# A hybrid decoder layer on one core: the end of its attention, with the conv branch evicted by VectorE and four pieces of work placed elsewhere

## The chip, the core and the metric

The kernel runs on one core of a Trainium2 chip. The core has a matrix engine (TensorE, PE in the profile, with its weight loads listed apart as PEld), VectorE (DVE), ScalarE (ACT), GpSimd (POOL) and SyncE (SP), which here issues nearly all transfers between the chip's main memory (HBM) and the on-chip memory (SBUF). Matrix products land in a small accumulator memory, PSUM, of eight banks of 128 x 512 float32 values; VectorE or ScalarE has to copy (evict) a bank before TensorE may write it again. Each engine works through its own list of instructions in order and waits on semaphores where it needs another's result. The metric is the device time of one execution in microseconds; lower is better.

## The reference, cut to what matters

One layer of a hybrid block on x (1024 positions, 1024 features). Two branches, attention and a gated causal convolution, are weighted by sigmoid gates, added and projected; a feed-forward block (FFN) with a convolution in it follows.

```
h = rms_norm(x, norm_mix_pre)
q, k, v, cb, cc, cx, g_att, g_conv = split(h @ w_in)       # 3 x 512, 3 x 512, 2 x 1024 columns
o = stick_breaking_attention(q, k, v)                       # 8 heads of 64, strictly causal
y_att  = o @ w_att_branch                                   # 512 -> 1024
y_conv = (cb * causal_dwconv(cc * cx, conv_mix_w)) @ w_conv_branch
merged = sigmoid(g_att) * y_att + sigmoid(g_conv) * y_conv
x = x + rms_norm(merged @ w_out, norm_mix_post)
h = rms_norm(x, norm_ffn_pre)
a, g = split(causal_dwconv(h @ w_up, conv_ffn_w))           # 2 x 2816
x = x + rms_norm((gelu(g) * a) @ w_down, norm_ffn_post)
```

In the attention the weight of a key s for a query t is exp(log_sigmoid(z) + the sum of log_sigmoid(-z) over the keys between s and t), so each block of keys needs a running sum from the blocks nearer to the query.

## The kernel before, in words

**Number format.** Every float32 operand of a product is scaled by a power of two and split into a float16 high part and a float16 low part (ScalarE writes the high part, VectorE the low part), and a product is three passes of float16 matmuls (high-high, low-high, high-low). The power of two comes from the operand's sum of squares: ScalarE squares the tile with an accumulator (`sumsq`, L58), VectorE casts the column of 128 sums to bf16 (`rb`), TensorE multiplies it by a matrix of ones (a 128 x 1 matmul into some PSUM bank), and VectorE turns the total into a scale with three tiny integer operations (`pow2_of`, L89 to L92, or `scale_of`, L78 to L81).

**The attention.** It works on units of two heads (j = 0 to 3), one half of the queries (c) and one block of 128 keys (i, downwards). A tile's name ends in the unit: `e3_11` is j = 3, c = 1, i = 1. For each unit TensorE makes scores z, ScalarE e = exp(z) (L804), VectorE bounds e (L813), ScalarE sp = log(1 + e) (L818), VectorE adds the running sum of the unit before (`sp <- A, sp`, L823), ScalarE and VectorE split sp into `sh` (L828, L832), TensorE sums it with a triangular matrix into A, ScalarE makes g = exp(-A) (L845), VectorE multiplies e by g (L849), and ScalarE and VectorE split the product into `w` (L854, L858), which TensorE multiplies by v into o. A has one PSUM buffer: the A of the next unit can be written only when g has read the last one. The last units, `3_13` to `3_10`, are the stretch of this case.

**The fills.** While that chain runs, TensorE is filled with projections that need nothing of it: q and k of the next heads, the three conv projections, the first gates gc and ga (`gate_fill`), and at the end, of the conv branch's eight output tiles d, d = 4 to 7 (`branch_fill`, `branch`, names `pywc4` to `pywc7` in PSUM, `ywc4` to `ywc7` in SBUF). Each is written into one of three PSUM banks; each bank's eviction is an operation (`Op`) in a list, and a small hand-written planner (`Side`) hands these operations out at fixed points of the attention's program, by a credit that each engine has there. The order that results is the order of the instructions on PE, DVE and ACT (a manual schedule). An `Op("sum", ...)` waits for the next bank that is evicted, and its 128 x 1 matmul uses that bank before the bank is given back; a first argument below zero puts it at the head of those that wait.

**p, the input of the conv branch.** Before `branch_fill(4)` the four tiles `pf0` to `pf3` have to be squared, their scale found (`p_ops`: `cast`, `total`, `scale`) and split into `p16_0` to `p16_3` (L715 on ScalarE, L719 on VectorE). `total` takes a bank of its own, `pr_p`.

**Weights.** `start_weight` fetches a weight tile into one of four buffers (`ws`) and lists square, cast, sum, high and low part for the planner. It does so for the list `wseq` up to an index `n_w`; its tail is wc2, wc3, wc0, wc1 (conv branch), wa0 to wa3 (attention branch). A fetch waits until the low part of the tile four places earlier is done, since that frees the buffer. What the planner leaves over is done by `prep`, by ordinary code behind the attention.

**After the attention.** The PSUM pools close and one pool of eight banks opens. `branch` then makes the conv branch's tiles d = 0 to 3, evicted by ScalarE (L769), with their squares right behind them, and the attention branch's eight tiles. Between them stand `blocks(0)` and `blocks(1)`: VectorE forms differences of blocks of h (tiles `T1` to `T4`, L1013 to L1017) and splits them into `hB` (L1003, L1004); the remaining gates g1 to g7 are then computed from them with fewer products (`pg1a`, `pg1b` and so on, TensorE L1539). Here the framework's scheduler sets the order of instructions, with its own estimates of time, and it may put such an instruction into the list of an engine among the attention's, when its inputs are there.

Of the kernel before, what the change touches and what calls it, by code (L numbers as in the profile page):

```python
# [20 lines left out]
AF = mybir.ActivationFunctionType  # L21
ALU = mybir.AluOpType
# [6 lines left out]
NH = 512  # L29
# [10 lines left out]
class Layer:  # L40
# [235 lines left out]
    def mixer(self, mid):  # L276
        tc, nc, a = self.tc, self.nc, self.a
        hT = self.hp.tile([P, 2, KD, T], F16, tag="hT", name="hT")
        with ExitStack() as ph1:
# [343 lines left out]
                while wpos[0] < n_w and wpos[0] - used[0] < ahead[0]:  # L623
                    start_weight()

            n_w = [i for i, (n_, _) in enumerate(self.wseq) if n_ == "wa1"][0] + 1
            ahead = [2]

            def need(name):
# [15 lines left out]
                yield from v_mm(tt)  # L645
                later(v_ops(tt, vps[tt]), True)

            cv, dep = {}, {}

            def conv_fill(j, which):  # L650
                w, inv = need(f"{which}{j}")
# [42 lines left out]
            def p_ops():  # L694
                st = {}
                acts[0] = [None] * 4

                def total():
                    st["ps"] = bank("pr_p")
                    q.total(st["ps"], st["rb"])  # L700

                def cast():
                    st["r"] = self.const.tile([P, 4], F32, tag="sp16", name="sp16", bufs=1)
                    st["rb"] = self.smp.tile([P, 1], BF16, tag="rb", name="rb_p", bufs=8)
                    nc.vector.tensor_reduce(st["r"][:, 0:1], smp_[:, 0:4], AX.X, ALU.add)
                    nc.vector.tensor_copy(st["rb"], st["r"][:, 0:1])

                def scale():
                    st["s"], inv_x[0] = self.pow2_of(st["r"], st["ps"])
                    parts()  # L710

                def high(j):
                    def f():
                        acts[0][j] = self.slot([P, 2, T], F16, f"p16_{j}")
                        nc.scalar.activation(acts[0][j][:, 0, :], pf[j], AF.Copy, scale=st["s"])  # L715
                    return f

                def low(j):
                    return lambda: nc.vector.scalar_tensor_tensor(acts[0][j][:, 1, :], pf[j], st["s"],  # L719
                                                                  acts[0][j][:, 0, :], ALU.mult, ALU.subtract)  # L720
                def parts():
                    for j in (3, 2, 1, 0):
                        later([Op("A", 1.1, high(j), soon=True), Op("V", 1.3, low(j), soon=True)], 2)
                return [Op("V", 0.3, cast, soon=True), Op(None, 0, total), Op("V", 0.5, scale, "pr_p", soon=True)]

            def gate_fill(which):
                w, inv = need(f"{which}0")
# [17 lines left out]
            def branch(bi, d, pm, later=None):  # L745

                which = ("wc", "wa")[bi]
                w, inv = self.wdone[f"{which}{d // 2}"] if later else self.prep(f"{which}{d // 2}")
                outs = []
                sc = sgn[:, 4 * bi + d // 2:4 * bi + d // 2 + 1]  # L750
                if d % 2 == 0:
                    self.mul(sc, inv_x[bi], inv)
                y = self.xp.tile([P, T], F32, tag="x", name=f"y{which}{d}") if (bi, d) in ((0, 0), (0, 1)) else \
                    self.slot([P, T], F32, f"y{which}{d}")
                for c in range(2):
                    ps = bank(f"py{which}{d}_{c}") if later else pm.tile([P, NH], F32, tag="pm", name=f"py{which}{d}_{c}")
                    n = 0
                    for k in range(4):
                        for wi, hi in PASSES:
                            nc.tensor.matmul(ps, w[0][:, wi, ds((d % 2) * NH + k * P, P)],  # L760
                                             acts[bi][k][:, hi, ds(c * NH, NH)], start=n == 0, stop=n == 11)
                            n += 1
                        yield
                    if later:
                        outs.append(Op("A", 0.6, lambda ps=ps, c=c: nc.scalar.activation(
                            y[:, ds(c * NH, NH)], ps, AF.Copy, scale=sc), f"py{which}{d}_{c}"))
                        later(outs[c:])
                    elif pm is self.pz:
                        nc.scalar.activation(y[:, ds(c * NH, NH)], ps, AF.Copy, scale=sc)  # L769
                    else:  # L770
                        nc.vector.tensor_scalar(y[:, ds(c * NH, NH)], ps, sc, None, ALU.mult)
                if later:
                    later([Op("A", 1.2, lambda: self.sumsq(y, smy[:, 8 * bi + d:8 * bi + d + 1], f"y{which}{d}"),
                              needs=outs)])
                else:
                    self.sumsq(y, smy[:, 8 * bi + d:8 * bi + d + 1], f"y{which}{d}")
                ys[which, d] = y
# [219 lines left out]
        with ExitStack() as ph2:  # L997
# [29 lines left out]
            def branches(*ds_, bi=1):  # L1027
                for d in ds_:
                    for _ in branch(bi, d, pm):
                        pass  # L1030
# [13 lines left out]
                m16.append(t)  # L1044

            branches(0, 1, bi=0)
            blocks(0)
            branches(2, 3, bi=0)
            self.pair_fetch("g1")
            self.inv_h = inv_h  # L1050
            blocks(1)
# [168 lines left out]
    def bank(self, name):  # L1220
        return self.pz.tile([P, NH], F32, tag="pm", name=name)
# [447 lines left out]
```

## Time and profile before

| quantity | value |
|---|---|
| time, median of 3 runs (lowest to highest) | 1355.66 us (1353.14 to 1358.48) |
| time of the profiled execution | 1352.85 us |
| span of the profiled execution | 1351.2 us |
| TensorE busy | 1311.1 us, 97% of the span |
| VectorE busy | 1047.4 us, 78% |
| ScalarE busy | 864.1 us, 64% |
| granted TensorE clock | 0.999 |

The profile shows one execution. A row of its timeline gives the start in us from the span's start, the duration, the engine, the line of the code, the operation, the tile written and the tiles read, shape and count, and in brackets the time for which the engine had been idle and who ended that idle time. A row of the waits gives who waited for whom, the sum in us, how often, and the longest. A row of the windows gives for a stretch the busy time of each engine, the granted clock, and what the DMA engines did. The program has three parts here: loading and normalizing up to some 60 us, the attention with its fills up to 426 us, and after that the branches, gates, output projection and FFN.

### The profile page before, as it was taken

How to read it: one execution, taken by the hardware profiler on the slowest of the kernel's cores; microseconds unless marked ns; L12 is line 12 of the kernel's file. 1: busy time of each engine (PE TensorE's matmuls, PEld its weight loads, DVE VectorE, ACT ScalarE, POOL GpSimd, SP SyncE). 2: the span in 40 equal slices, each digit the busy share in tenths (PEclk: the TensorE clock that was granted, in tenths of full speed). 3: DMA queues.
4: the chain of work that ended last, by engine and by line, in shares of the span. 5: the costliest groups of instructions: out<-in, count | busy, mean ns of one | idle time of the engine just before them, and what ended most of it. 6: DMA issues, size and time to landing. Idle time of an engine off the chain costs nothing. (4 is left out here: it accounts for less than half of the span.)

```text
span 1351.2 us, 16781 instructions
## 1 busy us (share of the span) xinstructions
PE 1311.1 (97%) x6491; PEld 589.9 (44%) x6491; DVE 1047.4 (78%) x1689; ACT 864.1 (64%) x1213; POOL 34.5 (3%) x58
## 2 busy tenths in 40 slices
PE   5999999999988999999999999999999999999997
PEld 3544444344433444444444444444444444444443
DVE  5578887878887857877788876985894896699855
ACT  6578778877788776675555676743752762576524
POOL 2000000000000000000110000000000000000002
PEclk9999999999999999999999999999999999999999
DMA  7111211101111122241331123122130322313126
GB/s 267 33 33 32 63 32 32 47 17 48 32 32 48 32 63 63 79 173 61 128 123 38 56 63 125 62 63 94 63 94 1 125 63 63 125 33 125 63 48 110
DMA packets 26608, 96.12 MB, mean 71 GB/s; under 512 B 3088, under 2 KB 3216, under 8 KB 26528
## 3 DMA queue, kind: packets, MB, share of 16 engines
q1 hardware_dynamic: 25088, 89.80, 20.3%
q0 software_dynamic: 1440, 5.24, 2.2%
q8 instruction: 51, 0.84, 0.3%
q14 instruction: 29, 0.24, 0.1%
HBM read 86.61 MB, written 8.42 MB: 70 GB/s over the span
## 5 line engine op out<-in xcount | busy, mean ns | idle before, releaser
L1539 PEld LDWEIGHTS <-wh_u 128*128 128x128 f16 x1848 | 178.8, 98 | 217.7 <-issue 4.0
L1313 PE MATMUL pd<-wdh,f 128*128 128x512 f16 (+1 forms) x1068 | 230.3, 377 | 2.7 <-ACT wdh L97 1.1
L1313 PEld LDWEIGHTS <-f 128*128 128x128 f16 x1068 | 104.4, 98 | 127.0 <-issue 4.0
L97 ACT ACTIVATE wh_u<-ws_u,sc 128x1024 f16<-128x1024 f32 (+1 forms) x66 | 64.7, 999 | 100.2 <-DVE sc L80 82.8
L1320 DVE SCALAR_TENSOR_TENSOR yacc<-pd,sd,yacc 128x512 f32<-128x512 f32 (+1 forms) x81 | 58.6, 742 | 72.9 <-PE pd L1313 65.4
L1539 PEld LDWEIGHTS <-wh_g 128*128 128x128 f16 x588 | 56.9, 98 | 68.6 <-issue 0.3
L1124 PE MATMUL py<-wh_wo,m 128*128 128x512 f16 x384 | 83.9, 379 | 0.0
L98 DVE SCALAR_TENSOR_TENSOR wh_u<-ws_u,sc,wh_u 128x1024 f16<-128x1024 f32 (+1 forms) x66 | 72.2, 1101 | 10.7 <-ACT wh_u L97 10.6
L828 ACT ACTIVATE sh<-sp 128x1024 f16<-128x1024 f32 (+3 forms) x48 | 40.4, 842 | 52.3 <-DVE sp L823 51.9
L1616 DVE SCALAR_TENSOR_TENSOR ugu<-cgu,cw_g,ugu 128x1023 f32<-128x1023 f32 (+1 forms) x44 | 56.4, 1281 | 11.3 <-ACT ugu L1614 10.9
L832 DVE TENSOR_TENSOR sh<-sp,sh 128x1024 f16<-128x1024 f32 (+3 forms) x48 | 45.8, 955 | 15.4 <-ACT sh L828 15.2
L1616 DVE SCALAR_TENSOR_TENSOR ua<-cau,cw_a,ua 128x1023 f32<-128x1023 f32 (+1 forms) x44 | 56.3, 1279 | 1.4 <-ACT ua L1614 1.3
L1124 PEld LDWEIGHTS <-m 128*128 128x128 f16 x384 | 37.5, 98 | 44.1
L823 DVE TENSOR_TENSOR sp<-A,sp 1x1024 f32<-1x1024 f32 (+3 forms) x40 | 35.9, 897 | 26.3 <-PE A L785 21.8
L858 DVE SCALAR_TENSOR_TENSOR w<-e,w 128x1024 f16<-128x1024 f32 (+3 forms) x48 | 45.8, 954 | 10.1 <-ACT w L854 9.9
L854 ACT ACTIVATE w<-e 128x1024 f16<-128x1024 f32 (+3 forms) x48 | 40.4, 843 | 17.4 <-DVE e L849 16.5
L818 ACT ACTIVATE sp<-e,one 128x1024 f32<-128x1024 f32 (+3 forms) x48 | 44.4, 925 | 6.0 <-DVE e L813 3.1
L849 DVE TENSOR_TENSOR e<-e,g 128x1024 f32<-128x1024 f32 (+3 forms) x48 | 45.7, 953 | 2.1 <-ACT g L845 2.0
L58 ACT ACTIVATE jk_u<-ws_u 128x1024 bf16<-128x1024 f32 x44 | 46.4, 1054 | 0.8
L211 PE MATMUL pcb<-hT,wh_cb 128*128 128x512 f16 x192 | 44.9, 380 | 0.9 <-DVE sc_cb L89 0.8
L804 ACT ACTIVATE e<-z,cz 128x1024 f32<-128x1024 f32 (+3 forms) x48 | 43.1, 897 | 3.6 <-PE z L785 3.6
L211 PE MATMUL pcc<-hT,wh_cc 128*128 128x512 f16 x192 | 45.1, 380 | 0.0
(705 smaller groups left out, 2620.6 us busy)
## 6 DMA issues: line engine op xcount, KB each, us to landing
ws_u<-w_up_nt SPq DMA_DIRECT2D x44, 512.0 KB
ds<-w_down SPq DMA_DIRECT2D x22, 512.0 KB
wd<-w_down SPq DMA_DIRECT2D x22, 512.0 KB
ws_g<-w_in_nt SPq DMA_DIRECT2D x14, 512.0 KB
x<-x SPq DMA_DIRECT2D x8, 512.0 KB
ws_wo<-w_out SPq DMA_DIRECT2D x8, 512.0 KB
xr<-x SPq DMA_DIRECT2D x8, 512.0 KB
out<-x SPq DMA_DIRECT2D x7, 512.0 KB
```

Source lines behind the costliest of these rows:

```text
L58: self.nc.scalar.activation(self.junk(f"jk_{name}"), src, AF.Square, accum_out=acc)
L97: self.nc.scalar.activation(dst[:, 0, :], src, AF.Copy, scale=s)
L98: self.nc.vector.scalar_tensor_tensor(dst[:, 1, :], src, s, dst[:, 0, :], ALU.mult, ALU.subtract)
L211: nc.tensor.matmul(ps, w[:, wi, ds(k * P, P)], hT[:, hi, k, ds(c * NH, NH)], start=n == 0, stop=n == last)
L832: nc.vector.tensor_tensor(sh[:, 1, :, off:], u["sp"][:, :, off:], sh[:, 0, :, off:], ALU.subtract)
L849: nc.vector.tensor_tensor(e[:, :, off:], e[:, :, off:], u["g"][:, :, off:], ALU.mult)
L858: nc.vector.scalar_tensor_tensor(w[:, 1, :, off:], u["e"][:, :, off:], 2.0 ** 14, w[:, 0, :, off:], ALU.mult, ALU.subtract)
L1124: nc.tensor.matmul(ps, m16[k][:, hi, ds(tt * P, P)], wo[k][:, wi, sl], start=k == 0 and p == 0, stop=k == 7 and p == 2)
L1313: nc.tensor.matmul(pd[nh], f16[g][k][:, hi, ds(tt * P, P)], w[k][:, wi, ds(*part)], start=run is runs[0] and n == 0, stop=run is runs[-1] ...
L1320: nc.vector.scalar_tensor_tensor(y[:, sl], ps, sm[:, 0:1], y[:, sl], ALU.mult, ALU.add)
L1539: nc.tensor.matmul(ps, w[wt][:, wi, ds(wc * NH + k * P, P)], self.block(i, hi, k), start=first and n == 0, stop=n == 3 * KH - 1, skip_grou ...
L1616: nc.vector.scalar_tensor_tensor(u[:, lag:], c[:, :T - lag], sm[:, 2 - lag:3 - lag], u[:, lag:], ALU.mult, ALU.add)
```

## The change

Five things are changed, all of them in the mixer:

1. The weight list that the planner works through ends at wc1 instead of wa1. The tiles wa0 and wa1 are fetched, squared and split by `prep`.
2. The total of p's squares no longer has the bank `pr_p`. It is an `Op("sum", -1, ...)`: it is made in the next bank that is evicted.
3. The conv branch's tiles d = 4 to 7 are evicted by VectorE (`tensor_scalar`, L762 of the new file) instead of ScalarE (L765 of the old one), with a planner's cost of 0.7 instead of 0.6.
4. The squares of these four tiles are not planned inside the attention; they are issued behind `branches(2, 3, bi=0)`.
5. The instructions of `blocks(0)` are told to come after the last of these evictions (`issue_after`).

```diff
-            n_w = [i for i, (n_, _) in enumerate(self.wseq) if n_ == "wa1"][0] + 1
+            n_w = [i for i, (n_, _) in enumerate(self.wseq) if n_ == "wc1"][0] + 1
...
-            cv, dep = {}, {}
+            cv, dep, tail, last = {}, {}, [], [None]
...
-                def total():
-                    st["ps"] = bank("pr_p")
-                    q.total(st["ps"], st["rb"])
...
-                def scale():
-                    st["s"], inv_x[0] = self.pow2_of(st["r"], st["ps"])
+                def scale(ps):
+                    st["s"], inv_x[0] = self.pow2_of(st["r"], ps)
                     parts()
...
-                return [Op("V", 0.3, cast, soon=True), Op(None, 0, total), Op("V", 0.5, scale, "pr_p", soon=True)]
+                return [Op("V", 0.3, cast, soon=True), Op("sum", -1, scale, st=st)]
...
                     if later:
-                        outs.append(Op("A", 0.6, lambda ps=ps, c=c: nc.scalar.activation(
-                            y[:, ds(c * NH, NH)], ps, AF.Copy, scale=sc), f"py{which}{d}_{c}"))
+                        def out(ps=ps, c=c):
+                            last[0] = nc.vector.tensor_scalar(y[:, ds(c * NH, NH)], ps, sc, None, ALU.mult)
+                        outs.append(Op("V", 0.7, out, f"py{which}{d}_{c}"))
                         later(outs[c:])
...
                 if later:
-                    later([Op("A", 1.2, lambda: self.sumsq(y, smy[:, 8 * bi + d:8 * bi + d + 1], f"y{which}{d}"),
-                              needs=outs)])
+                    tail.append(lambda: self.sumsq(y, smy[:, 8 * bi + d:8 * bi + d + 1], f"y{which}{d}"))
...
             branches(0, 1, bi=0)
-            blocks(0)
+            with tc.issue_after(last[0].ins):
+                blocks(0)
             branches(2, 3, bi=0)
+            for f in tail:
+                f()
```

Since the planner's list changes, instructions move on every engine at the end of the attention. Three places show it. A name there is the tile written, an arrow, and the tiles read; the last number of a tile's name is only a running number.

The first place is ScalarE's list around unit `3_12`, where p is split (`p16`) and the gates' banks are evicted (`sgc0`, `sga0`). Before:

```order
L854 ACTIVATE w3_14_3677<-e3_14_3521 128x1024
L715 ACTIVATE p16_0_3679<-pf0_1521,sp16_3603 128x1024
L715 ACTIVATE p16_1_3681<-pf1_2224,sp16_3603 128x1024
L715 ACTIVATE p16_2_3683<-pf2_2676,sp16_3603 128x1024
L818 ACTIVATE sp3_12_3701<-e3_12_3673,one_89 128x1024
L715 ACTIVATE p16_3_3713<-pf3_3377,sp16_3603 128x1024
L734 ACTIVATE sgc0_3534<-pgc0_1_3613,sc_gc0_3532 128x512
L828 ACTIVATE sh3_12_3749<-sp3_12_3701 128x1024
L845 ACTIVATE g3_13_3751<-A3_13_3725 128x1024
L734 ACTIVATE sga0_3687<-pga0_0_3688,sc_ga0_3685 128x512
L804 ACTIVATE e3_11_3756<-z3_11_3730,cz3_2994 128x1024
L854 ACTIVATE w3_13_3760<-e3_13_3597 128x1024
```

After:

```order
L850 ACTIVATE w3_14_3672<-e3_14_3521 128x1024
L814 ACTIVATE sp3_12_3691<-e3_12_3668,one_89 128x1024
L730 ACTIVATE sgc0_3534<-pgc0_1_3613,sc_gc0_3532 128x512
L824 ACTIVATE sh3_12_3736<-sp3_12_3691 128x1024
L841 ACTIVATE g3_13_3738<-A3_13_3713 128x1024
L711 ACTIVATE p16_0_3740<-pf0_1521,sp16_3603 128x1024
L711 ACTIVATE p16_1_3742<-pf1_2224,sp16_3603 128x1024
L711 ACTIVATE p16_2_3744<-pf2_2676,sp16_3603 128x1024
L800 ACTIVATE e3_11_3747<-z3_11_3718,cz3_2994 128x1024
L850 ACTIVATE w3_13_3751<-e3_13_3597 128x1024
L711 ACTIVATE p16_3_3756<-pf3_3377,sp16_3603 128x1024
L814 ACTIVATE sp3_11_3768<-e3_11_3747,one_89 128x1024
```

The four parts of p stand one unit later, behind the attention's `sh3_12` and `g3_13` and the eviction of `pgc0_1`; the evictions of `pga0_0` and `pga0_1` (not in the rows) follow `sp3_11`.

The second place is ScalarE's list around the last two units, with squares of weights (`jk_wa`), evictions and squares of the conv branch. Before:

```order
L854 ACTIVATE w3_12_3845<-e3_12_3673 128x1024
L58 ACTIVATE jk_wa0_0_3848,sm_wa0_3828<-ws_wa0_0_3826 128x1024
L818 ACTIVATE sp3_10_3860<-e3_10_3841,one_89 128x1024
L765 ACTIVATE ywc4_3821<-pywc4_0_3822,sgn_564 128x512
L828 ACTIVATE sh3_10_3895<-sp3_10_3860 128x1024
L845 ACTIVATE g3_11_3897<-A3_11_3881 128x1024
L765 ACTIVATE ywc4_3821<-pywc4_1_3856,sgn_564 128x512
L58 ACTIVATE jk_ywc4_3900,smy_565<-ywc4_3821 128x1024
L854 ACTIVATE w3_11_3904<-e3_11_3756 128x1024
L845 ACTIVATE g3_10_3954<-A3_10_3930 128x1024
L765 ACTIVATE ywc5_3886<-pywc5_0_3887,sgn_564 128x512
L765 ACTIVATE ywc5_3886<-pywc5_1_3920,sgn_564 128x512
```

After:

```order
L850 ACTIVATE w3_12_3827<-e3_12_3668 128x1024
L605 ACTIVATE wh_wc0_0_3829<-ws_wc0_0_3539,sc_wc0_3803 128x1024
L58 ACTIVATE jk_wc1_0_3831,sm_wc1_3684<-ws_wc1_0_3682 128x1024
L814 ACTIVATE sp3_10_3843<-e3_10_3823,one_89 128x1024
L58 ACTIVATE jk_wa0_0_4029,sm_wa0_4026<-ws_wa0_0_4027 128x1024
L58 ACTIVATE jk_wa1_0_4034,sm_wa1_4031<-ws_wa1_0_4032 128x1024
L824 ACTIVATE sh3_10_3877<-sp3_10_3843 128x1024
L841 ACTIVATE g3_11_3879<-A3_11_3863 128x1024
L58 ACTIVATE jk_wa2_0_4039,sm_wa2_4036<-ws_wa2_0_4037 128x1024
L850 ACTIVATE w3_11_3884<-e3_11_3747 128x1024
L841 ACTIVATE g3_10_3928<-A3_10_3911 128x1024
L850 ACTIVATE w3_10_3933<-e3_10_3823 128x1024
```

The evictions and squares of the conv branch are gone from here, and the scheduler has put the squares of three attention-branch weights (wa0, wa1, wa2) in their place, two of them between `sp3_10` and `sh3_10`.

The third place is VectorE's list where the attention ends (`o16` is the attention's last output tile). Before:

```order
L849 TENSOR_TENSOR e3_10_3841<-e3_10_3841,g3_10_3954 128x1024
L858 TENSOR_SCALAR w3_10_3961<-e3_10_3841,w3_10_3961 128x1024
L608 TENSOR_SCALAR wh_wa0_0_3963<-ws_wa0_0_3826,sc_wa0_3940,wh_wa0_0_3963 128x1024
L596 COPY rb_wa1_4006<-sm_wa1_3950 128x1
L1013 TENSOR_TENSOR T1_0_4149<-hT_102 128x1024
L1015 TENSOR_TENSOR T1_0_4149<-T1_0_4149,hT_102 128x1024
L1017 TENSOR_TENSOR T1_0_4149<-T1_0_4149,hT_102 128x1024
L878 TENSOR_SCALAR o16_3_3484<-o3_17_3545,o16_3_3484 128x512
```

After:

```order
L854 TENSOR_SCALAR w3_10_3933<-e3_10_3823,w3_10_3933 128x1024
L89 TENSOR_SCALAR sc_wc1_3963<-pywc5_1_3901 128x1
L91 TENSOR_SCALAR sc_wc1_3963<-sc_wc1_3963 128x1
L92 TENSOR_SCALAR sc_wc1_3963<-sc_wc1_3963 128x1
L762 TENSOR_SCALAR ywc6_3920<-pywc6_0_3921,sgn_564 128x512
L762 TENSOR_SCALAR ywc6_3920<-pywc6_1_3949,sgn_564 128x512
L101 TENSOR_TENSOR sgn_564<-sp16_3603,sc_wc1_3963 128x1
L608 TENSOR_SCALAR wh_wc1_0_3976<-ws_wc1_0_3682,sc_wc1_3963,wh_wc1_0_3976 128x1024
L762 TENSOR_SCALAR ywc7_3962<-pywc7_0_3967,sgn_564 128x512
L874 TENSOR_SCALAR o16_3_3484<-o3_17_3545,o16_3_3484 128x512
L762 TENSOR_SCALAR ywc7_3962<-pywc7_1_3985,sgn_564 128x512
L1009 TENSOR_TENSOR T1_0_4142<-hT_102 128x1024
```

The difference `T1` now begins behind the eviction of `pywc7_1`, where it had begun ahead of `o16`, and the evictions stand between the attention's own operations (those of `ywc5`, not in the rows, stand ahead of the multiplication that makes `e3_10`). wc1's scale is read here (`L89`) where wa0's low part stood.

On TensorE's list the number of matmuls is the same. The 128 x 1 total of p moves behind the second half of the gate gc (bank `pgc0_0`), wc0's total goes into `pgc0_1` instead of `pr_p`, wc1's into `pywc5_1` instead of `pga0_1`, the totals of wa0 and wa1 leave `pywc4_1` and `pywc7_0`, and those of wa0, wa1 and wa2 stand together behind the first tile of the conv branch after the attention. At the start of the FFN (tiles u1 to u3) the scheduler orders groups of matmuls differently, with the same instructions. SyncE's list has the same transfers in the same order.

## The prediction

> **What bounds the kernel now.** I read the page first, then the windows around the end of the attention, then the waits of TensorE there, and last the timeline, engine by engine.
>
> ```profile
> span 1351.2 us, 16781 instructions
> PE 1311.1 (97%) x6491; PEld 589.9 (44%) x6491; DVE 1047.4 (78%) x1689; ACT 864.1 (64%) x1213; POOL 34.5 (3%) x58
> ```
> ```profile
> 400.00:410.00 10.00, 7.57 (x40) 3.01 (x39) 8.36 (x11) 9.19 (x12) 0.00 (x0) 1.00 0.35 105
> ...
> 430.00:440.00 10.00, 7.77 (x39) 3.47 (x38) 8.12 (x11) 9.99 (x15) 0.00 (x0) 1.00 0.18 54
> 440.00:450.00 10.00, 10.00 (x48) 4.49 (x47) 9.60 (x16) 7.41 (x11) 0.00 (x0) 1.00 0.28 77
> ```
>
> TensorE is busy for all but 40.1 us of the span, at the full clock, and the change removes no matmul, so it can win or lose only through the gaps of TensorE. The windows (busy us of PE, PEld, DVE, ACT, POOL, with counts) show where those are: in the two ten-microsecond stretches that hold most of this change TensorE idles 2.4 and 2.2 us while ScalarE is busy 9.2 and 10.0 of 10; from 440 us on TensorE has no gap. The waits of TensorE between 366 and 470 us name every gap that the change can touch:
>
> ```profile
> PE pywc L1439 <- ACT ywc L765: 2.6, 1, 2.6
> PE pr L76 <- DVE rb L73: 2.2, 1, 2.2
> PE pr_p L1439 <- DVE rb_p L706: 1.8, 1, 1.8
> PE pga L211 <- ACT sgc L734: 1.3, 1, 1.3
> PE pga L1439 <- ACT sga L734: 0.8, 1, 0.8
> PE pywc L760 <- ACT ywc L765: 0.8, 1, 0.8
> ```
>
> Together 9.5 us, 0.7% of the span: no version of this stretch wins more. For what comes in their place I follow the new order on the three engines, each operation starting when its engine and its inputs are ready, with the durations of this trace. The same walk along the old order gives 10.0 us for the six waits, 0.5 too much.
>
> **1. p's total in an evicted bank, and p one unit later.** The total now stands behind the gate gc's second half, where its cast is long done: the 1.8 us go. The gate's eviction no longer stands behind p's high parts on ScalarE: the 1.3 go. The 0.8 (a weight's total that waited for the eviction of the last `pga` bank) go too, since that total has another bank, but the first conv tile needs the bank of `pga0_0`, whose eviction now follows `sp3_11`; the walk leaves 0.6. The price is that p itself is late.
>
> ```profile
> 382.48 3.21 ACT L715 ACTIVATE p<-pf,sp 128x1024 f16<-128x1024 f32 x3
> ...
> 383.75 3.67 DVE L719 SCALAR_TENSOR_TENSOR p<-pf,sp,p 128x1024 f16<-128x1024 f32 x3
> ...
> 388.70 1.28 DVE L719 SCALAR_TENSOR_TENSOR p<-pf,sp,p 128x1024 f16<-128x1024 f32 x1
> ...
> 391.14 1.12 ACT L804 ACTIVATE e<-z,cz 128x1024 f32<-128x1024 f32 x1
> ...
> 392.29 0.69 DVE L813 TENSOR_SCALAR e<-e 128x1024 f32<-128x1024 f32 x1
> ...
> 393.38 1.23 DVE L858 SCALAR_TENSOR_TENSOR w<-e,w 128x1024 f16<-128x1024 f32 x1
> ...
> 397.13 3.40 PE L760 MATMUL pywc<-p,wh_wc 128*128 128x512 f16 x15
> ```
>
> Before, p's last low part ended at 390.0 and its first reader started at 397.1: 7.1 us of cover. After, the walk has the first three high parts start at 386.5 on ScalarE; they (3.2) and the exponential `e3_11` (1.1) take it to 390.7; VectorE must bound `e3_11` (0.7, in order ahead of the low parts), then makes three low parts (3.7), the attention's `w` (1.2) and the fourth low part (1.3), to 397.5. TensorE, 3.2 us earlier than before, reaches the matmuls with the fourth part of p at 396.6: a new wait of 1.0. Part 1: -3.9 + 1.6 = -2.3.
>
> **2. Evictions of d = 4 to 7 on VectorE, three weight squares in the scheduler's hands.** The 2.6 us wait was a weight's total in `pywc4_1`, whose eviction stood behind `sh3_10` and `g3_11` on ScalarE. No total uses that bank now. What waits next is `A3_10`, one buffer, behind `g3_11`.
>
> ```profile
> 399.11 1.06 ACT L828 ACTIVATE sh<-sp 128x1024 f16<-128x1024 f32 x1 [2.05 <-DVE sp L823]
> 400.07 1.01 ACT L845 ACTIVATE g<-A 128x1024 f32<-128x1024 f32 x1
> ...
> 400.97 1.14 ACT L605 ACTIVATE wh_wc<-ws_wc,sc_wc 128x1024 f16<-128x1024 f32 x1
> ...
> 402.01 1.11 ACT L804 ACTIVATE e<-z,cz 128x1024 f32<-128x1024 f32 x1
> ...
> 403.01 1.06 ACT L854 ACTIVATE w<-e 128x1024 f16<-128x1024 f32 x1
> ...
> 403.96 1.05 ACT L58 ACTIVATE jk_wa<-ws_wa 128x1024 bf16<-128x1024 f32 x1
> ...
> 407.53 1.06 ACT L828 ACTIVATE sh<-sp 128x1024 f16<-128x1024 f32 x1 [0.81 <-DVE sp L823]
> ...
> 408.49 1.01 ACT L845 ACTIVATE g<-A 128x1024 f32<-128x1024 f32 x1
> ...
> 412.09 1.03 PE L785 MATMUL A<-sh,tri 128*128 128x512 f16 x4
> ```
>
> From `sh3_11` (399.1) to the end of `g3_11` (409.5) ScalarE took 10.4 us. After, `sh3_11` starts at the same 399.2 (it waits for VectorE, which has p's fourth part, 1.3, and the 1.2 of the running sum ahead of it). One eviction (0.7) and 0.8 of idling leave the stretch; an added weight square (1.05, and 0.15 for the next one to start), the idle time until VectorE has multiplied `e3_12` (0.6) and smaller waits come in, and wc1's square takes the place of its high part: 11.9 us, `g3_11` ends at 411.0. TensorE arrives at 408.2 (0.2 lost at `o` on the way, 0.4 at the triangular weights) and waits 2.9, and 0.1 more for `sh3_10`'s low part. So 2.6 go and 3.6 come: the two squares cost nearly what the total had.
>
> Behind it, VectorE's list is the one to read: the two evictions of `ywc5` now stand ahead of the multiplication of `e3_10`, and wc1's scale behind the `w3_10` that follows from it. wc1's total waits 0.2 for its bank's eviction, and `pywc7_0`, which needs that bank after VectorE has read the total, waits 1.0. Both are new. At the change to the pool of eight banks the 0.8 of before becomes 1.0, since `ywc7_1`'s eviction stands behind the attention's last low part. Part 2: -3.4 + 5.8 = +2.4.
>
> The price of one new eviction is in no row: `tensor_scalar` from PSUM, 128 x 512 float32.
>
> ```profile
> 365.70 0.74 DVE L667 SCALAR_TENSOR_TENSOR pf<-pcb,cv,pf 128x512 f32<-128x512 f32 x1
> ...
> 425.17 0.69 DVE L878 SCALAR_TENSOR_TENSOR o<-o,o 128x512 f16<-128x512 f32 x1 [1.54 <-ACT o L877]
> ```
>
> The upper end is 0.74 (two inputs, PSUM); the lower is half of the 0.69 that the same operation takes for 1024 elements out of SBUF, 0.35. I take 0.7, the nearest in size and source. At 0.4 the 0.2 and some 0.4 of the 1.0 vanish and the last reader comes 0.3 sooner: 0.9 us less in all; at 0.75, 0.15 more. [...]
>
> **3. wa0 and wa1 left to `prep`.** The 2.2 us wait was the total of wa2, whose square ScalarE reached at 432.9. After, the squares of wa0 to wa2 are done inside the attention (those of part 2), their totals stand behind the first tile after it, and wa3's cast has some 7 us in hand. All 2.2 go. The fetch of wa2 needs wc0's buffer, free at 406.9 in the walk; the square that waits for it is reached at 411.0, with the attention's `w3_11` behind it on ScalarE.
>
> ```profile
> 400.39 5.04 SPq L114 DMA_DIRECT2D ws_wa<-wa  x2
> ```
> ```profile
> 402.00:403.00 1.00, 1.00 (x7) 0.42 (x5) 0.67 (x1) 1.00 (x2) 0.00 (x0) 1.00 0.89 365
> 403.00:404.00 1.00, 1.00 (x6) 0.46 (x5) 0.84 (x2) 1.00 (x3) 0.00 (x0) 1.00 0.18 70
> ```
>
> The fetch issued at 400.4 moved its last bytes before 403.4, 3.0 us: landed at 409.9, 1.1 us in time. Beyond 4.1 us of transfer each microsecond is paid in full.
>
> **4. The differences behind the last eviction, the squares of y behind the branches.** Off TensorE's path, if what hides them holds: VectorE is full from 427 us on, and the first gate needs its products.
>
> ```profile
> 464.67 1.23 DVE L1004 TENSOR_TENSOR hB<-T,hB 128x1024 f16<-128x1024 f32 x1
> ...
> 472.53 2.48 DVE L98 SCALAR_TENSOR_TENSOR wh_g<-ws_g,sc,wh_g 128x1024 f16<-128x1024 f32 x2 [1.31 <-ACT wh_g L97]
> ...
> 480.96 2.75 PE L1539 MATMUL pg1a<-hT,wh_g 128*128 128x512 f16 x12
> ```
>
> Before, g1's first weight was split by 473.8 (two in 2.5 us from 472.5) and the last `hB` by 465.9, for products at 481.0. After, g1's fetches wait for wa0's and wa1's low parts (SyncE's queue: issued near 443 and 445 instead of 419.9 and 431.3), the four squares of y come ahead of g1's squares on ScalarE, and the walk has the first weight at 474.7 and the last `hB` near 471, for products at 478.5. The cover falls from 7.2 to 3.8 us, and it holds. Cost 0.
>
> **5. Groups of matmuls reordered in the FFN** (u1 to u3, from 733 us). Same instructions; the waits there:
>
> ```profile
> 770.02 2.75 PE L1539 MATMUL pu3a<-hA,wh_u 128*128 128x512 f16 x12 [0.26 <-ACT cgu L1554]
> ```
> ```profile
> PE pd L1313 <- DVE cau L1566: 1.0, 1, 1.0
> ...
> PE pd L1313 <- ACT wdh L97: 0.6, 1, 0.6
> ```
>
> At best their 1.9 us vanish, at worst they double; the first triple of `pu3a` now starts earlier and is split, so I put 0.3 on it.
>
> **Sum.** Removed 9.5. New 0.6 + 1.0 + 0.2 + 0.4 + 2.9 + 0.1 + 0.2 + 1.0 + 1.0 = 7.4, less the walk's excess of 0.5: 6.9. With 0.3 for the FFN: -2.3 us. The profiled execution (1352.85) would become 1350.6. It lies 2.8 under the median of the three runs, 1355.66, so as a median I forecast 1353.4.
>
> **Rivals.**
> - *More is won than the walk allows* (faster by over 0.5%, which is 6.8 us and about what a measurement of this kernel can tell from no change). It needs the two weight squares not to hold `g3_11`: then the 2.9 at `A3_10` shrinks to the 0.4 to 1 of its neighbours, with evictions at 0.4 another 0.9 goes, and the FFN gains up to 1.9: -2.3 - 2.2 - 0.9 - 1.9 = -7.3, 1348.4. Against it stand the order of the rows and three lucky ends at once. Chance 0.1.
> - *The gaps only change their name.* ScalarE and VectorE, not the banks, set the pace (9.2 and 8.4 of 10 busy at 400 us), and VectorE, with eight evictions more (5.5 us), delays `e3_10` and `w3_10` further than the walk has it. Each microsecond there is one at `pywc7_0` and one at the attention's last output; 1.2 us twice take back everything: 1355.7, no change. For it: part 2 is already a loss. Chance 0.27.
> - *Slower: the first gate waits.* From some point VectorE's list behind the attention (differences, four weight splits, merges) is the bound. It decides when VectorE is 3.8 us later than in the walk; beyond it every microsecond is TensorE's. Slower than before from 6.1 us late, and by over 0.5% from 12.9 us late. The walk has the tail 4.8 us later than before (four differences out of the attention); if the eight evictions lengthen it in full, that is 5.6 more, and if the four squares of y find no idle time on ScalarE ahead of g1's squares, another 4.8: 10.4 us late, 1355.7 + 10.4 - 6.1 = 1360.0. Against it: VectorE also loses wa0's and wa1's low parts in the attention (2.6) and idles there. With late fetches on top it passes 1362.4. Chance 0.1, and 0.07 for over 0.5%.
>
> **How the numbers follow.** The likeliest, 0.53, is the sum, with -0.5 to -4.5 as its own range (evictions at 0.4 to 0.75, the FFN from -1.9 to +1.9): 1351.2 to 1355.2. The runs before spread 2.8 to either side of their median, which I add in part, and the range takes in the second rival: 1348.5 to 1358.5. Over 0.5% faster than 1355.66 is below 1348.9: the first rival and the edge of the main case, 0.12. Over 0.5% slower, above 1362.4: 0.08 with what I have not thought of. The rest, 0.8, is no change that can be told.
>
> **What would show it.** Right: the waits of TensorE lose `pr_p`, `sgc`, `ywc` and `rb`; new ones stand at `A` behind ScalarE's `g` (near 3 us), at the fourth part of p (near 1) and at `pywc` behind `sc_wc`; nothing waits at `pg1a`; L762 takes near 0.7 us. Wrong: a wait at `pg1a` or at its weights; a ScalarE idle before `jk_wa` on a transfer; L762 near 0.4; new waits of several microseconds after 700 us.

## The result, and the profile after

The changed kernel takes 1350.92 us as the median of its first seven executions and 1351.66 us as that of twelve later ones; the kernel before took 1355.82 and 1355.28 beside them. Both times the ratio is 0.997, with a 95% interval of 0.9962 to 0.9985 and of 0.9962 to 0.9984. By the ratio that is 3.7 us faster (the medians themselves lie 4.9 and 3.6 apart), less than the 0.5% that I had called telling, and yet clear of no change. The forecast was 1353.4 as a median. 1350.92 lies 0.3 below the 1351.2 to 1355.2 that I had given the likeliest case by itself, and 1351.66 inside it; the whole range, 1348.5 to 1358.5, holds both.

The two profiled executions stand closer together than the medians: 1352.85 and 1350.92 us. This is the page of the changed kernel, then the waits of TensorE between 366 and 470 us (in total, times, longest), then two of the windows that the prediction showed of before.

```profile
span 1349.2 us, 16783 instructions
PE 1311.9 (97%) x6491; PEld 590.0 (44%) x6491; DVE 1050.8 (78%) x1697; ACT 859.1 (64%) x1205; POOL 34.5 (3%) x58
```
```profile
PE A L781 <- ACT g L841: 3.0, 1, 3.0
PE pywc L756 <- ACT sga L730: 1.1, 1, 1.1
PE pywc L756 <- DVE ywc L762: 0.8, 1, 0.8
PE pywc L756 <- DVE sc_wc L89: 0.8, 1, 0.8
PE pywc L756 <- DVE p L715: 0.7, 1, 0.7
```
```profile
400.00:410.00 10.00, 8.15 (x40) 3.41 (x39) 8.01 (x8) 9.46 (x13) 0.00 (x0) 1.00 0.18 53
430.00:440.00 10.00, 10.00 (x52) 4.60 (x50) 9.97 (x18) 7.93 (x10) 0.00 (x0) 1.00 0.01 2
```

None of the six old waits is left as it was; five others make 6.4 us in place of 9.5. At 430 us TensorE no longer waits for a total. At 400 us one stall stands in place of another, 3.0 us at `A` instead of 2.6 at `pywc4_1`; it runs past the end of the window, which shows 1.9 us of it.

Where the time went is best measured between two fixed points: the first matmul of q behind the loading of the weights, and the first of gate 1. Timeline and tile of TensorE, before and then after:

```profile
43.62 3.62 PE L211 MATMUL pq<-hT,wh_q 128*128 128x512 f16 x16
```
```profile
L1539 PE MATMUL pg1a<-hT,wh_g x24: 379/379/379, 481.0 to 491.1; 128*128 128x512 f16 x24
```
```profile
44.16 3.18 PE L211 MATMUL pq<-hT,wh_q 128*128 128x512 f16 x14
```
```profile
L1538 PE MATMUL pg1a<-hT,wh_g x24: 379/379/379, 479.0 to 489.1; 128*128 128x512 f16 x24
```

Before, 481.0 - 43.62 = 437.4 us; after, 479.0 - 44.16 = 434.8: the stretch is 2.5 us shorter. The waits became 3.1 shorter by the rows above, 2.9 by the hundredths of the timeline; what takes back the last 0.3 is open. The loading ahead of it happened to take 0.5 longer, so the times stay 1.9 apart; behind gate 1 both traces take 870.2 us. The table below gives this stretch for every kernel, so that the loading, which scatters by 1.6 us among the fourteen traces (q starts between 43.6 and 45.3), is left out.

### The profile page after: what moved, and what is told of

Same layout as the page of the kernel before. It is cut to its first block, busy times and chain, and to the rows that moved or that the text cites. A ratio compares the mean times of both kernels' runs of the same rounds, so it can differ in the third digit from the quotient of the medians.

```text
span 1349.2 us, 16783 instructions
## 1 busy us (share of the span) xinstructions
PE 1311.9 (97%) x6491; PEld 590.0 (44%) x6491; DVE 1050.8 (78%) x1697; ACT 859.1 (64%) x1205; POOL 34.5 (3%) x58
## 5 line engine op out<-in xcount | busy, mean ns | idle before, releaser
L819 DVE TENSOR_TENSOR sp<-A,sp 1x1024 f32<-1x1024 f32 (+3 forms) x40 | 35.9, 897 | 25.4 <-PE A L781 21.7
L756 PE MATMUL pywc<-p,wh_wc 128*128 128x512 f16 x192 | 43.2, 379 | 3.5 <-ACT sga L730 1.1
```

## The experiments

The first question was whether the terms of the sum belong to the parts of the change. Parts are numbered as in the prediction: 1 is p, 2 the evictions, 3 the limit of the weight list, 4 the differences and the squares of y. Four kernels undo one part of the changed kernel, three make one part alone in the kernel before, one is the kernel before again. No kernel undoes the later squares of y by themselves, and none makes part 4 alone. The waits are the sums of the printed rows.

| kernel | median us | ratio to before, 95% | waits 366 to 470 us | q to gate 1, us |
|---|---|---|---|---|
| before (its runs beside the others) | 1355.0 to 1355.8 | 1 | 9.5 | 437.4 |
| same_again | 1354.78 | 0.999 to 1.001 | 9.5 | 437.4 |
| changed | 1350.92 | 0.996 to 0.999 | 6.4 | 434.8 |
| changed_again | 1351.66 | 0.996 to 0.998 | 5.6 | 435.0 |
| undo_p | 1355.07 | 0.999 to 1.001 | 7.7 | 437.4 |
| undo_evict | 1354.37 | 0.999 to 1.001 | 8.1 | 437.4 |
| undo_wa | 1349.81 | 0.995 to 0.998 | 5.2 | 435.0 |
| undo_hold | 1354.29 | 0.998 to 1.001 | 7.0 | 436.3 |
| only_p | 1354.83 | 0.999 to 1.001 | 7.9 | 438.8 |
| only_evict | 1355.09 | 0.999 to 1.001 | 9.2 | 438.9 |
| only_wa | 1357.54 | 1.001 to 1.003 | 10.3 | 440.7 |
| evict_filled | 1354.64 | 0.999 to 1.001 | 4.1 | 436.6 |
| squares_late | 1350.42 | 0.995 to 0.998 | 5.6 | 434.0 |
| wa_filled | 1350.35 | 0.996 to 0.998 | 4.4 | 434.6 |

**undo_p**: p's total in its own bank again.

```diff
...
+                def total():
+                    st["ps"] = bank("pr_p")
+                    q.total(st["ps"], st["rb"])
...
-                return [Op("V", 0.3, cast, soon=True), Op("sum", -1, scale, st=st)]
+                return [Op("V", 0.3, cast, soon=True), Op(None, 0, total), Op("V", 0.5, scale, "pr_p", soon=True)]
```

> The changed kernel with one part undone: p's total again in a bank of its own. Theory 1, that each part of the change carries its own waits, as the prediction's sum has them: the waits at pr_p (1.8), at pga behind sgc (1.3) and behind sga (0.8) come back, the 1.1 behind sga at pywc and the 0.7 behind the fourth part of p go: +2.1 us, span 1351.3. Theory 2, that ScalarE's and VectorE's lists set the pace and a wait that goes is paid again further on: the walk has waits of 1.6, 0.7 and 1.6 there, 3.3 at A3_10 behind g3_11 and none at the three places behind it, +0.8 us in all, span 1350.0.

```profile
PE A L785 <- ACT g L845: 2.0, 1, 2.0
PE pga L1442 <- ACT sga L734: 1.8, 1, 1.8
PE pr_p L1442 <- DVE rb_p L702: 1.8, 1, 1.8
PE pga L211 <- ACT sgc L734: 1.3, 1, 1.3
PE pywc L760 <- DVE ywc L766: 0.8, 1, 0.8
```

The old waits are back (1.8, 1.3, and 1.8 instead of 0.8), the one at `A` is 2.0 instead of 3.0 and the one behind sc_wc is gone: +1.3 in all, between theory 2's 0.8 and theory 1's 2.1. But the stretch is 2.5 longer than the changed kernel's, which no sum of waits explains. The reason comes below, and with it the reading changes: this run does not decide between the two.

**undo_evict**: ScalarE evicts d = 4 to 7 again.

```diff
-                            last[0] = nc.vector.tensor_scalar(y[:, ds(c * NH, NH)], ps, sc, None, ALU.mult)
-                        outs.append(Op("V", 0.7, out, f"py{which}{d}_{c}"))
+                            last[0] = nc.scalar.activation(y[:, ds(c * NH, NH)], ps, AF.Copy, scale=sc)
+                        outs.append(Op("A", 0.6, out, f"py{which}{d}_{c}"))
```

> The changed kernel with d = 4 to 7 evicted by ScalarE again, all else as changed. Theory 1 (parts): part 2 lost 2.4 by the prediction and 1.3 by the changed kernel's trace (3.0 + 0.8 + 0.9 of new waits against 3.4 removed), so undoing it wins 1.3 to 2.4 us: span 1346.8 to 1347.9. Theory 2 (lists): ScalarE, already the later one there, gets eight evictions back; the walk has one wait of 4.7 at pywc4_1 behind ywc4's eviction in place of the 2.9 at A, 1.1 behind sc_wc and 1.3 at the pool change: +1.6 us, span 1350.8.

```profile
PE pywc L1438 <- ACT ywc L762: 5.1, 1, 5.1
PE pywc L756 <- DVE o L874: 1.2, 1, 1.2
```

The wait that the walk put at 4.7 is there with 5.1, and the waits are 1.7 longer, near the 1.6 of theory 2. To undo the part that the prediction had charged with a loss of 2.4 loses: theory 1 falls.

**undo_wa** and **undo_hold**: the limit of the planner back to wa1; the differences free again.

```diff
-            n_w = [i for i, (n_, _) in enumerate(self.wseq) if n_ == "wc1"][0] + 1
+            n_w = [i for i, (n_, _) in enumerate(self.wseq) if n_ == "wa1"][0] + 1
```
```diff
-            with tc.issue_after(last[0].ins):
-                blocks(0)
+            blocks(0)
```

> The changed kernel with wa0 and wa1 prepared inside the attention again. Theory 1 (parts): the wait of 2.2 for a weight's total behind the attention comes back: +2.2 us, span 1351.4. Theory 2 (lists): ScalarE is free of the evictions of y, so wa2's square is in time anyway; the walk has 2.0 at A3_10 instead of 2.9, 1.1 at pywc7_0, 0.3 at a total behind sc_wa0 and 1.4 at the pool change, none at pr behind rb: -0.1 us, span 1349.1.

> The changed kernel with the gate differences free to stand inside the attention again; the squares of y stay behind the branches. Theory 1 (parts): part 4 costs and wins nothing, span 1349.2, the wait at the pool change stays 0.9. Theory 2 (lists): the differences stand ahead of ywc7_1's eviction on VectorE; the walk has 2.6 there instead of 1.05: +1.5 us less 0.2 further on, span 1350.5.

```profile
PE A L781 <- ACT g L841: 2.2, 1, 2.2
PE pywc L756 <- DVE ywc L762: 1.2, 1, 1.2
```
```profile
PE A L781 <- ACT g L841: 3.0, 1, 3.0
PE pywc L756 <- DVE ywc L762: 2.2, 1, 2.2
```

Both lists hold beside these rows only the 1.1 behind sga and the 0.7 behind p. Undoing part 3 brings no wait at `pr` back and makes the kernel, if anything, faster (1349.81). Undoing part 4 makes the wait at the pool change 2.2 instead of 0.8 and costs 1.4 us of the stretch, near theory 2's 1.5. Its median lies some 3 us above the changed kernel's, more than that wait explains.

**The parts alone** (the same edits, made in the kernel before), and the kernel before again.

> The kernel before, unchanged, profiled a second time. If its first profile lay 2.8 us under the median of its runs because executions scatter, this one's span may lie anywhere from 1351 to 1356, the same six waits of TensorE between 366 and 470 us stand at the same places within 0.3 us each, and what differs lies in the loading of the first 45 us or behind 700 us. If the profiled execution is always the faster one, the span is 1351.2 within 0.5 again.

> The kernel before with p's total in the evicted bank, nothing else changed. Theory 1 (parts): -2.3 us by the prediction, -2.1 by the changed kernel's trace, span 1348.9 to 1349.1. Theory 2 (lists): 3.9 of waits go, but p's lateness and ScalarE's list give most of it back; the walk has 0.6, 1.0, then 5.0 at pywc4_1 behind ywc4's eviction (2.6 before), 1.6 and 1.3 at the pool change: -0.6 us, span 1350.6.

> The kernel before with d = 4 to 7 evicted by VectorE, nothing else changed (squares of y planned inside the attention, differences not held back). Theory 1 (parts): part 2's +2.4 without the two weight squares that the planner's new limit brings in, some +0.3: span 1351.5. Theory 2 (lists): VectorE's list becomes the later one; the walk has 2.5 at pywc4_1, 1.4 at pywc6_0 and 4.4 at the pool change behind ywc7's eviction: +2.7 us, span 1353.9.

> The kernel before with wa0 and wa1 left to prep, nothing else changed. Theory 1 (parts): the 2.2 at pr behind rb go, -2.2 us, span 1349.0. Theory 2 (lists): the 2.6 at pywc4_1 go too, since no total uses that bank, but ScalarE now has the squares of y and of wa0 to wa3 behind the attention; the walk has three waits at pr behind rb, 1.3, 3.6 and 1.2, in place of the one of 2.2: +0.6 us, span 1351.8.

Of each the waits that tell:

```profile
PE pywc L1435 <- ACT ywc L761: 4.9, 1, 4.9
PE pywc L756 <- DVE sc_wa L89: 1.2, 1, 1.2
```
```profile
PE pywc L760 <- DVE ywc L765: 2.3, 1, 2.3
PE pywc L760 <- DVE sc_wa L89: 1.6, 1, 1.6
```
```profile
PE pr L76 <- DVE rb L73: 4.6, 2, 3.4
```

The second profile of before shows the same six waits to the tenth, and again an execution some 2 us under the median. No part alone wins: only_p turns the 2.6 at pywc4_1 into 4.9, only_wa turns one wait at `pr` into three (1.2 and 3.4 in the row, and 1.0 behind `sc`, not shown). The walk was right on the places in these two. On only_evict it was too dark: it had 4.4 at the pool change, the trace 2.3.

**A drop of the clock.** The waits leave 1 to 3 us unexplained in most of these kernels. The windows show why: of the traces, those of before, same_again and the changed kernel are the only ones of these ten in which the granted clock (the third number from the end) is 1.00 in this whole stretch. In undo_evict and, below it, only_wa:

```profile
410.00:415.00 5.00, 2.77 (x8) 1.03 (x8) 2.67 (x4) 4.97 (x8) 0.00 (x0) 0.69 0.09 32
```
```profile
433.00:436.00 3.00, 0.34 (x3) 0.23 (x3) 2.96 (x9) 3.00 (x7) 0.00 (x0) 0.57 0.00 0
436.00:439.00 3.00, 3.00 (x8) 1.06 (x7) 1.95 (x7) 2.97 (x5) 0.00 (x0) 0.50 0.00 0
439.00:442.00 3.00, 3.00 (x12) 1.24 (x11) 3.00 (x7) 3.00 (x4) 0.00 (x0) 0.79 0.02 5
```

In the other seven it stands at 0.50 behind a stall, for 3 to 7 us (in windows of 1 us from 412 to 415 us in undo_evict, from 434 to 440 us in only_wa): eight matmuls in 3 us in the middle row of only_wa, where the window from 440 us of the kernel before had 48 in ten. The mean clock of an execution hints at it without a trace, but coarsely: the changed kernel's trace holds no drop, changed_again's (below) holds one, and both have 0.998. Of 98 executions of the kernel before, 28 have a mean clock of 0.999 (median 1352.88 us), 11 of 0.998 (1355.02), 47 of 0.997 (1355.44) and 12 of 0.995 (1358.35). Both profiled executions (1352.85 and 1352.93) had 0.999. In only_evict the order is the other way, though: 1355.2 at 0.999 (four executions) and 1354.1 at 0.997 (three), so the mean clock does not sort the times of every kernel.

This also changes the reading of undo_p. Its trace has a drop behind its stall of 2.0 us at `A`:

```profile
414.00:417.00 3.00, 3.00 (x9) 1.14 (x9) 1.88 (x3) 1.54 (x2) 0.00 (x0) 0.65 0.00 0
```

A drop takes the place of the wait behind sc_wc (changed_again, below). Against the changed kernel's trace with such a drop, 5.6 us, undo_p's 7.7 are 2.1 more; and at a mean clock of 0.998 the median of its three executions is 1353.1, that of the changed kernel's eleven 1351.0. Both differences are theory 1's 2.1, so in the changed kernel part 1 may well be worth what the sum gave it, though `A`'s wait did move, as theory 2 has it. The traces of the other three hold such a drop too: against the same 5.6 us undo_evict is 2.5 longer, undo_hold 1.4 longer and undo_wa 0.4 shorter, so there theory 1 (1.3 to 2.4 shorter, no change, 2.2 longer) stays wrong.

Four more kernels followed from the drops.

**changed_again**: the changed kernel, unedited. **evict_filled** and **wa_filled**: matmuls that nobody reads, put into a wait of undo_evict and of undo_wa.

```diff
...
+            def fill_pe(n):
+                zz = pat.tile([P, 2, NH], F32, tag="z", name="zz")
+                for _ in range(n):
+                    mm(zz[:, 0, :], hT[:, 0, 0, 0:P], hT[:, 0, 0, 0:NH], start=True, stop=True)
...
             def sums(u):
                 off, sh = u["off"], u["sh"]
+                fill_pe(8) if u is units[-1] else None
```

(wa_filled; evict_filled has `fill_pe(20)` ahead of the total in pywc4_1 instead.)

> The changed kernel, unchanged, in more executions. The eight runs so far show that the granted clock halves for 3 to 7 us behind a stall of TensorE in some executions, and that the first traces of the kernel before and of the changed kernel hold no such drop between 60 and 1340 us. Theory 3: the change's gain of 3.7 to 4.9 us in the medians is 2.0 of shorter waits and the rest drops of the clock that the kernel before has in most executions and the changed kernel in few; then its median is 1350.9 again, at most a quarter of its executions lie above 1352, and the waits are 1.1, 0.7, 3.0, 0.8 and 0.8 again. Rival: the first seven executions were lucky; the 3.0 us stall at A3_10 drops the clock as often as the stalls of before do, and the median is 1352.5 to 1353.

> The kernel undo_evict (ScalarE evicts d = 4 to 7) with 20 matmuls more that nobody reads, 128 x 512, right ahead of the total that waits 5.1 us for pywc4_1's eviction: they keep TensorE busy for 4.3 of those 5.1 us and release nothing sooner. Theory 3 (an idle TensorE loses its clock): the wait in the trace shrinks to 0.8, the clock stays at 1.00 from 405 to 420 us, and the median falls from 1354.4 by the 1.7 to 2.0 us that 3.4 to 4 us at half clock cost: 1352.4 to 1352.7. Rival (the drop has another cause, such as the load itself): the drop stays, and the median is 1354.4 or more.

> The kernel undo_wa (wa0 and wa1 inside the attention, the other three parts as changed) with 8 matmuls more that nobody reads, 128 x 512, ahead of A3_10: they fill 1.7 of the 2.2 us for which TensorE waits there. Theory 3: the wait shrinks to 0.5, the clock stays at 1.00 from 405 to 420 us in every execution, the median is that of undo_wa's undisturbed executions, 1349.5 to 1350.0, and none lies above 1351 for a drop there; faster than the changed kernel by 1 us. Rival: the drop does not follow idleness, and executions of 1351.7 stay; or A3_10 now starts later, at most 0.5 us.

The window from 410 to 415 us, of evict_filled, wa_filled and changed_again:

```profile
410.00:415.00 5.00, 3.64 (x17) 1.58 (x17) 3.03 (x7) 4.97 (x9) 0.00 (x0) 1.00 0.00 0
```
```profile
410.00:415.00 5.00, 4.50 (x21) 1.84 (x19) 4.00 (x7) 2.80 (x3) 0.00 (x0) 1.00 0.08 33
```
```profile
410.00:415.00 5.00, 2.84 (x7) 1.02 (x7) 3.04 (x8) 4.51 (x8) 0.00 (x0) 0.66 0.17 70
```

That the idle time cost the clock at this wait is shown: with the wait filled, evict_filled's clock is 1.00 where undo_evict's is 0.69, and undo_evict had a mean clock of 0.996 in nine of ten executions, evict_filled has 0.997 to 0.999 in all twelve, with 20 matmuls more (some 4.3 us). What it is worth was wrong. The median did not fall (1354.64 against 1354.37), the stretch became 0.8 shorter and not 1.7 to 2.0, because the wait behind sc_wc came back (the 0.6 is what was left of the filled one, the 0.8 stands for the 1.2 at the pool change):

```profile
PE pywc L756 <- DVE sc_wc L89: 0.9, 1, 0.9
PE pywc L756 <- ACT ywc L762: 0.8, 1, 0.8
...
PE pywc L1447 <- ACT ywc L762: 0.6, 1, 0.6
```

At 412 us the drop in undo_evict ate slack that TensorE otherwise waits away (the 0.9 behind sc_wc). changed_again says the same: its trace has a drop there, and its stretch is 435.0 against 434.8, since the 0.8 behind sc_wc is gone. In only_wa the drop at 433 us is paid: waits 0.8 above those of before, the stretch 3.3 longer, so 2.5 for the drop; behind it TensorE has no wait to shorten until 640 us. wa_filled missed too: the wait at A fell to 0.5, but two of eight executions still took 1352.8 at a mean clock of 0.997, so drops elsewhere seem to remain (the traces of undo_p, undo_evict and evict_filled have one near 725 us, behind the start of the FFN). In undo_p, the stall and the window behind it:

```profile
724.33 0.38 PE L1542 MATMUL pu0c<-hB,wh_u 128*128 128x512 f16 x1 [1.79 <-ACT hB L1159]
```
```profile
726.00:729.00 3.00, 3.00 (x9) 1.10 (x8) 3.00 (x6) 2.09 (x4) 0.00 (x0) 0.51 0.00 0
```

The same stall of 1.8 us stands in all fourteen traces, and eleven of them lose no clock behind it.

changed_again has the same ratio again (0.9973), but misses its expectation in the details: the median is 1351.66 and not 1350.9, four of twelve executions lie above 1352 where it had at most three, two of them by 0.1, and the stall at `A` dropped the clock in its trace. Over its 19 executions the changed kernel has 16 between 1350.2 and 1352.1 (median 1351.0) and three at 1353.0 to 1354.8 with a clock of 0.996 or 0.995; of the 98 of the kernel before, 69 lie above 1353.9.

**squares_late**: the squares of wa0 to wa2 behind the attention's last high part on ScalarE (`gi` holds the instructions of the high parts).

```diff
-            branches(0, 1, bi=0)
+            with tc.issue_after(gi["3_10"].ins): branches(0, 1, bi=0)
```

> The changed kernel with the squares of wa0 to wa2 held behind the attention's last high part (w3_10) on ScalarE; nothing else moves there but the small copies that follow from them. The prediction's claim, that the two squares between sp3_10 and sh3_10 cost nearly what the total had: the wait of 3.0 at A3_10 falls by their 2.1 us to 0.9, span 1347.1. Theory 2 (lists): sh3_10 cannot start before A3_11 has been summed and carried over, so ScalarE stood idle without the squares for most of one of them; the walk leaves 2.2 at A3_10 (the same as in undo_wa), span 1348.4, and no new wait for a weight's total.

ScalarE and the wait at A, of the changed kernel and then of squares_late:

```profile
405.94 1.14 ACT L814 ACTIVATE sp<-e,one 128x1024 f32<-128x1024 f32 x1
406.98 1.04 ACT L58 ACTIVATE jk_wa<-ws_wa 128x1024 bf16<-128x1024 f32 x1
...
408.14 1.06 ACT L58 ACTIVATE jk_wa<-ws_wa 128x1024 bf16<-128x1024 f32 x1
...
409.20 1.04 ACT L824 ACTIVATE sh<-sp 128x1024 f16<-128x1024 f32 x1
410.14 1.00 ACT L841 ACTIVATE g<-A 128x1024 f32<-128x1024 f32 x1
```
```profile
408.80 1.06 ACT L824 ACTIVATE sh<-sp 128x1024 f16<-128x1024 f32 x1 [1.28 <-DVE sp L819]
409.76 1.01 ACT L841 ACTIVATE g<-A 128x1024 f32<-128x1024 f32 x1
```
```profile
410.82 1.16 PE L781 MATMUL A<-sh,tri 128*128 128x512 f16 x4 [2.22 <-ACT g L841]
```

Without the squares ScalarE idles 1.28 us until VectorE has added the row of A3_11 into sp3_10 (L819). The wait is 2.2, as theory 2 had it, not 0.9; the stretch is 0.8 shorter. With a ratio of 0.9962 (0.995 to 0.9975) squares_late and, at the same ratio, undo_wa are the fastest kernels run; their intervals overlap the changed kernel's, so their times do not show that they beat it; for squares_late the stretch of its one trace speaks for it.

## Why the prediction was right, and where it was not

**The sum.** 6.9 us of waits were forecast and 6.4 came: behind sga 1.1 (0.6 forecast), at the fourth part of p 0.7 (1.0), at A 3.0 (2.9), behind sc_wc 0.8 (1.0), at the pool change 0.8 (1.0); the four small ones (0.2, 0.4, 0.1, 0.2) did not come. The sum was -2.3; the trace has -2.5 in the stretch and -1.9 in the time, with 0.5 of later loading. That the terms stand where the walk put them, each within 0.5, bears out the walk; that the totals agree to 0.4 is partly luck, since the 0.9 of small terms that did not come is offset by the 0.5 that I had taken off and by longer waits behind sga. The range, ten us wide, would have held no change as well, so that the median fell into it says little.

**The median.** The step that failed is "it lies 2.8 under the median of the three runs, so as a median I forecast 1353.4": it took for a constant what, by the mean clocks, is a drop of the clock that most executions of the kernel before pay (59 of 98 are at 0.997 or less) and few of the changed kernel do (four of 19). Among executions without a large drop (16 of the changed kernel, 28 of the kernel before) the difference is 1351.0 - 1352.88 = -1.9; at 0.999 on both sides it is 1350.6 (four executions) - 1352.88 = -2.3. The other 1.4 to 1.8 of the 3.7 us go with the clock. So "it can win or lose only through the gaps of TensorE" fell short too: the full clock of the one profiled execution was that of 28 in 98, and a gap can also cost by what follows it. Where the drops of the kernel before lie is open, since neither of its traces holds one. The stall at the start of the FFN stands in the changed kernel as well; of the others, 2.6 at `pywc4_1` and 2.2 at `pr`, the one at `pr` has no slack behind it and is the likelier, as in only_wa, whose drop came behind 3.4 us there. That is argued, not shown.

**The parts.** The sums by part (-2.3, +2.4, -2.2, 0) were bookkeeping, not worth of the parts. Part 1 costs about its 2.3 when undone (2.1 by the comparisons above), yet wins nothing alone. Undoing part 2 costs time instead of winning 2.4; part 3 wins nothing, since with the other parts in place no wait at `pr` comes back without it; part 4, put at 0, saves 1.4 at the pool change by its differences. Parts 1, 2 and 4 win only together: with any one of them taken out (of part 4 the differences) the median is within 1 us of before, and parts 1 and 2 alone win nothing.

**The squares.** "The two squares cost nearly what the total had" is wrong in size: 0.8 of their 2.1. With that the first rival falls, which needed the wait at A to shrink to 0.4 to 1: the chain from A3_11 over the carried row to `g3_11` alone keeps 2.2.

**Evictions.** I took 0.7 for the new one, with 0.75 as the upper bound; the tile's row (shortest, median and longest in ns) has 0.745:

```profile
L762 DVE TENSOR_SCALAR ywc<-pywc,sgn x8: 741/745/751, 405.1 to 426.2; 128x512 f32<-128x512 f32 x8
```

One input costs here what the row with two inputs out of PSUM cost (0.74). On ScalarE the same evictions took 0.06 less in the kernel before:

```profile
L765 ACT ACTIVATE ywc<-pywc,sgn x8: 667/682/691, 406.0 to 426.0; 128x512 f32<-128x512 f32 x8
```

**The cover.** `pg1a` waits for nothing (no wait of TensorE between 470 and 640 us). Its first weight, one of two in this row of the changed kernel, is split by 474.2 (474.7 forecast):

```profile
472.96 2.48 DVE L98 SCALAR_TENSOR_TENSOR wh_g<-ws_g,sc,wh_g 128x1024 f16<-128x1024 f32 x2 [1.67 <-ACT wh_g L97]
```

With products at 479.0 the cover is 4.8 us, 3.8 forecast, so the slower rival has no place, and the third square of wa starts at 411.05 with ScalarE never idle before it, so wa2's fetch was in time. In the FFN the wait at `pu3a` (0.3) vanished and two others grew, from 0.7 and 0.6, so 0.1 in place of the 0.3 that I had put there:

```profile
PE pu0a L1538 <- ACT cgu L1553: 1.0, 1, 1.0
PE pd L1312 <- ACT wdh L97: 0.7, 1, 0.7
```

## What to carry to other kernels

A wait belongs to the order of the work, not to the instruction beside it: price a change as a whole by following the lists of all engines, and don't sell its parts singly. Before a profiled execution is compared with medians, look at the mean granted clock of the executions: for the kernel before it splits them into groups 2.5 to 3 us apart, as much as the change itself. And when two traces are compared wait by wait, see first whether both hold a drop in that stretch. A stall can cost more than its length when a drop follows it: here a drop of some 3 us with a wait of 0.8 us behind it to use up made the stretch 0.2 us longer (changed_again), one of some 7 us with none behind it 2.5 us longer, beside its waits (only_wa).

## What the hardware showed unexpectedly

The granted clock fell to about 0.50 behind stalls of TensorE of 1.8 us (the one at `pu0c`, in three traces of fourteen), of 2.0 us (undo_p) and 2.2 us (undo_wa's trace; squares_late's, with as long a stall there, holds none), of 3.0 us (changed_again's trace has it, the changed kernel's has not, at the same stall) and of 4.9 us (only_p's trace; all ten of its executions have a mean of 0.996 or 0.997). The length of a stall alone does not decide it: the 1.8 us at `pu0c` left the clock at 1.00 in eleven traces of fourteen, and the two stalls of 2.6 and 2.2 us of the kernel before left it at 1.00 in both of its traces. What decides it no run here shows.
